# Rotary embedding on one core: all work in pairs of rows, and three PSUM banks for TensorE

## The chip, the core and the metric

The kernel runs on one core of a Trainium2 chip. The metric is the device time of one execution in microseconds (us); of several runs the median is given. The engines are TensorE (PE, its weight loads PEld), VectorE (DVE), ScalarE (ACT), GpSimd (POOL) and SyncE (SP), which here only issues transfers. Data come from and go to the chip's memory by sixteen DMA engines.

## What is computed

```python
def reference(x, cos, sin, num_heads):          # x: (16, 512, 1024), cos and sin: (512, 32), 16 heads
    batch, seq, dim = x.shape
    head_dim = dim // num_heads                 # 64
    half_dim = head_dim // 2                    # 32
    x = x.reshape(batch, seq, num_heads, head_dim)
    x1, x2 = (x[..., :half_dim].copy(), x[..., half_dim:].copy())
    cos = cos[None, :, None, :].copy()
    sin = sin[None, :, None, :].copy()
    return np.concatenate([x1 * cos - x2 * sin, x1 * sin + x2 * cos], axis=-1)
```

All is float32. Each element is used once: 33.6 MB are read and 33.6 MB written.

## The kernel before

The input is cut into eight tiles of 4 MB. A tile holds two batches: 128 partitions with eight rows of 1024 elements each (R = 8). Five buffers (`NB`, line 35) hold tiles, so the load of tile 5 goes into the buffer of tile 0 and has to wait until that one is stored.

In each row the result is x * cos + swapped(x) * signed sin, where "swapped" exchanges the two halves of each head. So a row costs two multiplications and an addition. The names in the code:

- `T` and `B` (line 157) are the second product, swapped(x) * sin. GpSimd makes nearly all of them; one is made by VectorE. `T1` and `T2` cover three rows each, `B` the remaining two.
- `P` (line 171) is the first product, x * cos, put by VectorE into a PSUM tile `pp`. `S` (line 174) adds the two, `T + pp`, back into the tile, also on VectorE.
- `A` (line 168) is the first product in place, for the two rows whose addition is left to TensorE. TensorE adds by multiplying both products with an identity matrix into one PSUM tile `ps` of 512 columns (lines 188 and 189), and ScalarE copies it back (line 190). One such step is called a chunk here; a pair of rows has four. Five tiles (`ONPE`) do so with their pair: twenty chunks. There is one bank `ps`, so a chunk begins when the copy of the one before is done.

The order is written out by hand: `GPO` for GpSimd, `DVO` for VectorE. `CARRY` and `AHEAD` add waits by hand, so that an engine's later instructions need none of their own, and the memset `both` (line 206) stands behind GpSimd's first `T` to carry the wait for the tables. The cosine and sine tables are spread over the partitions by a matmul each (line 117); cosine stays in PSUM (`cos_ps`).

All transfers of x are in SP's queue, in this order: the loads of tiles 0 to 4 (tile 0 in three pieces, tile 1 in two), the stores of tiles 0 to 2, the loads of tiles 5 to 7, the stores of tiles 3 to 7 (the last in two pieces). SP issues one after the other and waits at each for what it needs. The two tables are loaded from ScalarE's queue.

Of the kernel before, what the change touches and what calls it, by code (L numbers as in the profile page):

```python
# [7 lines left out]
FP32 = mybir.dt.float32  # L8
ALU = mybir.AluOpType
# [3 lines left out]
def kernel(  # L13
# [8 lines left out]
    nc = tc.nc  # L22
    P = nc.NUM_PARTITIONS
    batch, seq, dim = x.shape
    nh = num_heads
    hd = dim // nh
    half = hd // 2


    BP = 2  # L30
    HP = P // BP
    R = seq // HP
    NT = batch // BP
    assert HP * R == seq and BP * NT == batch
    NB = 5
    G = 3

    ROWS = {"1": (0, G), "2": (G, G), "pair": (2 * G, R - 2 * G)}

    LAST = {"pair": (0, R - 2 * G), "1": (R - 2 * G, G), "2": (R - G, G)}  # L40

    ONPE = (1, 3, 4, 5, 6)

    GPO = [("T1", "T2")] + [("B", "T1", "T2") if t in (2, 4, 7) else ("T1", "B", "T2") for t in range(1, NT)]

    DVO = [("P1", "S1", "P2", "B", "S2", "P3", "S3"), ("A", "P1", "S1", "P2", "S2"),
           ("P1", "S1", "P2", "S2", "P3", "S3"), ("A", "P1", "S1", "P2", "S2"), ("P1", "S1", "P2", "A", "S2"),
           ("P1", "S1", "P2", "A", "S2"), ("P1", "A", "S1", "P2", "S2"), ("P3", "S3", "P1", "S1", "P2", "S2")]

    CARRY = {(0, "P1"): "both", (0, "P2"): "T2", (1, "A"): "B", (3, "A"): "B", (4, "A"): "T2", (5, "P1"): "T1", (5, "A"): "T2",  # L50
             (6, "A"): "B", (7, "P3"): "B"}

    AHEAD = (1, 2, 3, 5)

    xv = x.rearrange("b (p r) d -> (b p) (r d)", r=R)
    xv = xv.rearrange("(t p) f -> t p f", p=P)
    ov = out.rearrange("b (p r) h d -> (b p) (r h d)", r=R)
    ov = ov.rearrange("(t p) f -> t p f", p=P)
# [2 lines left out]

    fixed = ctx.enter_context(tc.tile_pool(name="fixed", bufs=1))
    xin = ctx.enter_context(tc.tile_pool(name="xin", bufs=1))
    tpool = ctx.enter_context(tc.tile_pool(name="tpool", bufs=2))
    bpool = ctx.enter_context(tc.tile_pool(name="bpool", bufs=2))
    ptab = ctx.enter_context(tc.tile_pool(name="ptab", bufs=1, space=bass.MemoryType.PSUM))
    pgrp = ctx.enter_context(tc.tile_pool(name="pgrp", bufs=1, space=bass.MemoryType.PSUM))
    prow = ctx.enter_context(tc.tile_pool(name="prow", bufs=1, space=bass.MemoryType.PSUM))

    ctx.enter_context(tc.manual_schedule())  # L70

    SYNC = mybir.DependencyInfo(mybir.DependencyClass.Sync, mybir.DependencyReason.DATA)

    def implied(inst, *others):

        for o in others:
            tc.declare_no_dep(inst.ins, o.ins, reason="implied by an earlier wait of the engine")


    bufs = [xin.tile([P, R * dim], FP32, name=f"x{i}_sb") for i in range(NB)]  # L80
    x_tiles = [bufs[t % NB] for t in range(NT)]
    loads = [None] * NT
    stores = [None] * NT
    copies = [[] for _ in range(NT)]
    H = dim // 2

    def load(t, cuts=(0, 2 * R)):
        loads[t] = [nc.sync.dma_start(out=x_tiles[t][:, a * H:b * H], in_=xv[t][:, a * H:b * H])  # L88
                    for a, b in zip(cuts, cuts[1:])]

    def store(t, *parts):
        stores[t] = [nc.sync.dma_start(out=ov[t][:, a * H:b * H], in_=x_tiles[t][:, a * H:b * H])
                     for a, b in parts or ((0, 2 * R),)]

    load(0, (0, 1, 2 * G, 2 * R))
    tabs = fixed.tile([HP, 2, R * half], FP32, name="tabs")
    nc.scalar.dma_start(out=tabs[:, 1], in_=sinv)
    nc.scalar.dma_start(out=tabs[:, 0], in_=cosv)
    load(1, (0, 2 * G, 2 * R))
    for t in range(2, NB):  # L100
        load(t)


    ident = fixed.tile([P, P], FP32, name="ident")
    nc.gpsimd.memset(ident, 0.0)  # L105
# [6 lines left out]
    nc.gpsimd.tensor_copy(out=sel.rearrange("k (b p) -> k b p", b=BP),  # L112
                          in_=bass.AP(tensor=i64.tensor, offset=i64.offset, ap=[i64.ap[0], [0, BP], [1, HP]]))

    cos_ps = ptab.tile([P, R, half], FP32, name="cos_ps")
    sin_ps = pgrp.tile([P, G * dim], FP32, name="pp")[:, :R * half].rearrange("p (r j) -> p r j", r=R)
    spread = [nc.tensor.matmul(out=o.rearrange("p r j -> p (r j)"), lhsT=sel, rhs=tabs[:, i],  # L117
                               start=True, stop=True) for i, o in ((1, sin_ps), (0, cos_ps))]

    PR, PN = ROWS["pair"]  # L120
    sns = fixed.tile([P, R, 2, half], FP32, name="sns")
    snp = prow.tile([P, dim // 2], FP32, name="ps")
    signed = []
    for o, r0 in ((sns, 0), (snp[:, :PN * hd].rearrange("p (r s j) -> p r s j", r=PN, s=2), PR)):
        signed.append(nc.scalar.copy(out=o[:, :, 1, :], in_=sin_ps[:, r0:r0 + o.shape[1], :]))  # L125
        signed.append(nc.scalar.mul(out=o[:, :, 0, :], in_=sin_ps[:, r0:r0 + o.shape[1], :], mul=-1.0))  # L126

    def view(ap, r0, n):

        return ap[:, r0 * dim:(r0 + n) * dim]  # L130

    def cosb(r0, n):
        return bass.AP(tensor=cos_ps.tensor, offset=cos_ps.offset + r0 * half,
                       ap=[cos_ps.ap[0], [half, n], [0, 2 * nh], [1, half]])

    def snsb(tab, r0, n):

        return bass.AP(tensor=tab.tensor, offset=tab.offset + r0 * hd,
                       ap=[tab.ap[0], [hd, n], [0, nh], [1, hd]])

    def swapped(xt, r0, n):
        return bass.AP(tensor=xt.tensor, offset=xt.offset + r0 * dim + half,
                       ap=[xt.ap[0], [hd, n * nh], [-half, 2], [1, half]])

    Ts, TIs = {}, {}
    both = fixed.tile([1, 1], FP32, name="both")

    def span(t, o):
        return (LAST if t == NT - 1 else ROWS).get(o[-1]) or (LAST if t == NT - 1 else ROWS)["pair"]

    def second(eng, t, o):

        r0, n = span(t, o)
        pool = bpool if o == "B" else tpool
        Ts[t, o] = pool.tile([P, n * dim], FP32, name=o[0])
        tab = snsb(snp, r0 - PR, n) if eng is nc.vector else snsb(sns, r0, n)
        TIs[t, o] = eng.tensor_tensor(out=Ts[t, o], in0=swapped(x_tiles[t], r0, n), in1=tab, op=ALU.mult)  # L157
        return TIs[t, o]

    pps = {}  # L160

    def vector(t, o):
        r0, n = span(t, o)
        xr = view(x_tiles[t], r0, n)
        if o == "B":
            i = second(nc.vector, t, o)
        elif o == "A":
            i = nc.vector.tensor_tensor(out=xr, in0=xr, in1=cosb(r0, n), op=ALU.mult)  # L168
        elif o[0] == "P":
            pps[o[1]] = pgrp.tile([P, G * dim], FP32, name="pp")[:, :n * dim]  # L170
            i = nc.vector.tensor_tensor(out=pps[o[1]], in0=xr, in1=cosb(r0, n), op=ALU.mult)  # L171
        else:
            T = Ts[t, "B" if o == "S3" else "T" + o[1]]
            i = nc.vector.tensor_tensor(out=xr, in0=T, in1=pps[o[1]], op=ALU.add)  # L174
        if (t, o) in CARRY:
            after(i, TIs[t, CARRY[t, o]])
        implied(i, *loads[t], *spread, *signed)
        if t >= NB:
            implied(i, *loads[t - NB], *stores[t - NB], *copies[t - NB])
        return i  # L180

    def pe_rows(t):

        xr = view(x_tiles[t], PR, PN)
        for c in range(2 * PN):
            ps = prow.tile([P, dim // 2], FP32, name="ps")
            xc = xr[:, c * H:(c + 1) * H]
            nc.tensor.matmul(out=ps, lhsT=ident, rhs=xc, start=True, stop=False)  # L188
            nc.tensor.matmul(out=ps, lhsT=ident, rhs=Ts[t, "B"][:, c * H:(c + 1) * H], start=False, stop=True)  # L189
            i = nc.scalar.copy(out=xc, in_=ps)  # L190
            implied(i, *loads[t], *([As[t]] if t in As else []))
            if t >= NB:
                implied(i, *loads[t - NB], *stores[t - NB], *copies[t - NB])
            copies[t].append(i)

    def after(inst, other):
        tc.add_manual_dep(inst.ins, other.ins.name, SYNC, reason="brings the wait to the engines behind")

    As = {}

    def compute(t):
        for o in GPO[t]:
            i = second(nc.gpsimd, t, o)
            if (t, o) == (0, "T1"):

                TIs[0, "both"] = nc.gpsimd.memset(both, 0.0)  # L206
                after(TIs[0, "both"], signed[-1])
                after(TIs[0, "both"], spread[1])
        for o in DVO[t]:
            i = vector(t, o)  # L210
            if o == "A":
                As[t] = i
        if t in ONPE:
            pe_rows(t)

    for t in range(NB):
        compute(t)
# [5 lines left out]
        store(t)  # L223
    for t in range(NB, NT):
        compute(t)
        if t == NT - 1:
            store(t, (0, 2 * (R - G)), (2 * (R - G), 2 * R))
        else:
            store(t)
    for t in AHEAD:  # L230
        for l in loads[t + 1]:
            after(TIs[t, "T2"], l)


# [33 lines left out]
```

## Time and profile before

| | |
|---|---|
| median of three runs | 164.04 us (162.93 to 164.66) |
| span of the profiled execution | 162.0 us (no other time of this execution is given) |
| VectorE busy | 134.1 us, 83% |
| GpSimd busy | 138.9 us, 86% |
| TensorE busy | 54.6 us, 34%, 84 records |
| ScalarE busy | 14.0 us, 9% |
| DMA | 67.24 MB, mean 415 GB/s |

The span reaches from the first to the last instruction of one execution taken by the profiler. Busy times are sums of one engine's instructions; the engines work beside each other, so they don't add up to the span. A line of the profile's groups names the source line, the engine, the operation with its output and inputs, the shape, how often it ran, then its busy time, the mean of one in ns, and the idle time just before it.

### The profile page before, as it was taken

The numbers are of one execution on the slowest core, as the hardware profiler recorded it, in microseconds if no ns is written. First come the engines' busy times: TensorE is split into PE (matmuls) and PEld (weight loads), VectorE is DVE, ScalarE is ACT, GpSimd is POOL, SyncE is SP. The second block draws the span as 40 slices with busy tenths as digits, with TensorE's granted clock in tenths as the row PEclk, the third lists the DMA queues.
The fourth block names the chain that finished last, engine by engine and source line by source line (L and its number), as shares of the span: only waits on it lengthen the run. The fifth ranks groups of instructions, "written<-read, shape, count | busy, mean of one in ns | idle before, by whom it ended". The sixth has DMA issues, their size and how long they took to land.

```text
span 162.0 us, 381 instructions
## 1 busy us (share of the span) xinstructions
PE 54.6 (34%) x84; PEld 18.0 (11%) x84; DVE 134.1 (83%) x44; ACT 14.0 (9%) x25; POOL 138.9 (86%) x31
## 2 busy tenths in 40 slices
PE   0230000008680000038640009863988686400000
PEld 0110000002220000022110002220222132100000
DVE  0004999999999999999999999998968999999800
ACT  3200000000211000001210000021011212100000
POOL 2199999979999999999999999999999999992000
PEclk9999999999998555556995555599555899975555
DMA  6999999999999999998999999998999999799995
GB/s 190 392 456 403 425 496 388 461 445 388 461 445 388 404 502 388 421 485 388 429 453 396 445 461 396 461 437 372 453 445 404 396 396 453 332 388 518 384 409 243
DMA packets 3040, 67.24 MB, mean 415 GB/s; under 512 B 352, under 2 KB 480, under 8 KB 608
## 3 DMA queue, kind: packets, MB, share of 16 engines
q1 hardware_dynamic: 2880, 67.11, 97.2%
q10 hardware_dynamic: 160, 0.13, 0.2%
HBM read 33.69 MB, written 33.55 MB: 415 GB/s over the span
## 4 chain that ended last, share of the span: by engine, by line
DVE 33%; issue 26%; PE 19%; POOL 8%; ACT 4%; DMA 4%; SPq 0%; DVEq 0%; POOLq 0%
DVE x_sb L174 15%; DVE pp L171 13%; PE ps L188 11%; PE ps L189 9%; POOL T L157 6%; ACT x_sb L190 4%; DMA x_sb<-in_x_dram 4%; POOL B L157 3%; DVE x_sb L168 3%; DVE B L157 1%; SPq L88 0%; POOL both L206 0%; POOLq L157 0%; DVEq L174 0%; DVEq L171 0%
## 5 line engine op out<-in xcount | busy, mean ns | idle before, releaser
L157 POOL TENSOR_TENSOR T<-x_sb,sns 128x3072 f32<-128x3072 f32 x16 | 107.0, 6717 | 7.2 <-DMA x_sb<-in_x_dram 6.9
L171 DVE TENSOR_TENSOR pp<-x_sb,cos_ps 128x3072 f32<-128x3072 f32 (+1 forms) x19 | 60.7, 3193 | 15.2 <-POOL both L206 14.4
L188 PE MATMUL ps<-x_sb,ident 128*128 128x512 f32 x40 | 29.0, 815 | 76.6 <-issue 39.6
L174 DVE TENSOR_TENSOR x_sb<-T,pp 128x3072 f32<-128x3072 f32 x16 | 53.6, 3352 | 1.0
L157 POOL TENSOR_TENSOR B<-x_sb,sns 128x2048 f32<-128x2048 f32 x7 | 31.9, 4561 | 0.0
L189 PE MATMUL ps<-B,ident 128*128 128x512 f32 x40 | 26.7, 756 | 0.0
L190 ACT COPY x_sb<-ps 128x512 f32<-128x512 f32 x20 | 11.7, 585 | 121.9 <-PE ps L189 121.9
L188 PEld LDWEIGHTS ps<-x_sb,ident 128*128 128x128 f32 x40 | 7.4, 231 | 98.1 <-issue 68.8
L168 DVE TENSOR_TENSOR x_sb<-x_sb,cos_ps 128x2048 f32<-128x2048 f32 x5 | 11.4, 2285 | 2.8 <-POOL B L157 2.2
L189 PEld LDWEIGHTS ps<-B,ident 128*128 128x128 f32 x40 | 9.7, 241 | 13.4 <-issue 13.4
L174 DVE TENSOR_TENSOR x_sb<-B,pp 128x2048 f32<-128x2048 f32 x3 | 6.9, 2286 | 0.1
L117 PE MATMUL pp<-tabs,sel 64*128 64x256 f32 x2 | 1.2, 694 | 4.3 <-DMA tabs<-in_sin_dram 4.3
L117 PE MATMUL cos_ps<-tabs,sel 64*128 64x256 f32 x2 | 1.2, 713 | 4.1 <-DMA tabs<-in_cos_dram 4.1
L157 DVE TENSOR_TENSOR B<-x_sb,ps 128x2048 f32<-128x2048 f32 x1 | 2.3, 2281 | 0.0
L125 ACT ACT_TABLE_LOAD x1 | 1.3, 1283 | 1.9 <-issue 1.9
L117 PEld LDWEIGHTS cos_ps<-tabs,sel 64*128 64x128 f32 x2 | 0.5, 308 | 4.8 <-DMA tabs<-in_cos_dram 4.8
L117 PEld LDWEIGHTS pp<-tabs,sel 64*128 64x128 f32 x2 | 0.5, 310 | 4.3 <-issue 4.3
L125 ACT COPY sns<-pp 128x256 f32<-128x256 f32 x1 | 0.4, 372 | 2.3 <-PE pp L117 2.3
L105 POOL MEMSET ident<- 128x128 f32 x1 | 0.2, 204 | 0.3 <-POOLq L249 0.3
L126 ACT ACTIVATE sns<-pp 128x256 f32<-128x256 f32 x1 | 0.4, 390 | 0.0
L106 POOL TENSOR_SCALAR_AFFINE_SELECT ident<-ident 128x128 f32<-128x128 f32 x1 | 0.3, 292 | 0.1
L112 POOL COPY sel<-ident 64x128 f32<-64x128 f32 x1 | 0.3, 282 | 0.1
(7 smaller groups left out, 1.0 us busy)
## 6 DMA issues: line engine op xcount, KB each, us to landing
out_dram<-x_sb SPq DMA_DIRECT2D x7, 4096.0 KB, 20.5
x_sb<-in_x_dram SPq DMA_DIRECT2D x6, 4096.0 KB, 30.2
x_sb<-in_x_dram SPq DMA_DIRECT2D x2, 2560.0 KB, 16.4
out_dram<-x_sb SPq DMA_DIRECT2D x1, 2560.0 KB, 11.1
x_sb<-in_x_dram SPq DMA_DIRECT2D x1, 1536.0 KB, 15.2
out_dram<-x_sb SPq DMA_DIRECT2D x1, 1536.0 KB, 7.9
x_sb<-in_x_dram SPq DMA_DIRECT2D x1, 1280.0 KB, 6.3
x_sb<-in_x_dram SPq DMA_DIRECT2D x1, 256.0 KB, 3.0
```

Source lines behind the costliest of these rows:

```text
L106: nc.gpsimd.affine_select(out=ident, in_=ident, compare_op=ALU.not_equal, fill=1.0, base=0, pattern=[[-1, P]], channel_multiplier=1,)
L112: nc.gpsimd.tensor_copy(out=sel.rearrange("k (b p) -> k b p", b=BP), in_=bass.AP(tensor=i64.tensor, offset=i64.offset, ap=[i64.ap[0], [0, ...
L117: spread = [nc.tensor.matmul(out=o.rearrange("p r j -> p (r j)"), lhsT=sel, rhs=tabs[:, i], start=True, stop=True) for i, o in ((1, sin_ps ...
L125: signed.append(nc.scalar.copy(out=o[:, :, 1, :], in_=sin_ps[:, r0:r0 + o.shape[1], :]))
L126: signed.append(nc.scalar.mul(out=o[:, :, 0, :], in_=sin_ps[:, r0:r0 + o.shape[1], :], mul=-1.0))
L157: TIs[t, o] = eng.tensor_tensor(out=Ts[t, o], in0=swapped(x_tiles[t], r0, n), in1=tab, op=ALU.mult)
L168: i = nc.vector.tensor_tensor(out=xr, in0=xr, in1=cosb(r0, n), op=ALU.mult)
L171: i = nc.vector.tensor_tensor(out=pps[o[1]], in0=xr, in1=cosb(r0, n), op=ALU.mult)
L174: i = nc.vector.tensor_tensor(out=xr, in0=T, in1=pps[o[1]], op=ALU.add)
L188: nc.tensor.matmul(out=ps, lhsT=ident, rhs=xc, start=True, stop=False)
L189: nc.tensor.matmul(out=ps, lhsT=ident, rhs=Ts[t, "B"][:, c * H:(c + 1) * H], start=False, stop=True)
L190: i = nc.scalar.copy(out=xc, in_=ps)
```

## The change

Everything is done in pairs of rows (`G = 2`), four pairs in a tile, and one list `PLAN` holds the order for all engines. `T` is the second product on GpSimd, `B` the same on VectorE, `P` and `S` as before, `A` the first product in place and `M` the four chunks of a pair on TensorE with ScalarE's copies. Odd tiles give GpSimd three pairs and VectorE one `B`; even tiles from 2 on give GpSimd all four. Tiles 1 to 6 have two `M` each, tile 7 has one.

The second products share a ring of five buffers (`tpool`), the chunks a ring of three PSUM banks (`prow`). The cosine table and the part of the sine table that VectorE needs share one bank (`tab`). In a chunk the second product's matmul now stands ahead of the first's. The waits by hand (`CARRY`, `AHEAD`, `both`) are gone; each instruction waits for what it reads and overwrites.

Tile 0 is loaded in pieces of 2, 2 and 4 rows, the other tiles in one piece, and the last store is cut after six rows. The order of the transfers in SP's queue stays otherwise.

```diff
-    G = 3
-    ROWS = {"1": (0, G), "2": (G, G), "pair": (2 * G, R - 2 * G)}
-    ONPE = (1, 3, 4, 5, 6)
-    GPO = [("T1", "T2")] + [("B", "T1", "T2") if t in (2, 4, 7) else ("T1", "B", "T2") for t in range(1, NT)]
-    DVO = [("P1", "S1", "P2", "B", "S2", "P3", "S3"), ("A", "P1", "S1", "P2", "S2"),
...
+    G = 2
+    C = 512
+    PLAN = ["T0 P0 T1 S0 B3 P1 S1 T2 P3 S3 P2 S2",
+            "T0 T1 A0 M0 B3 T2 A1 M1 P3 S3 P2 S2",
+            "T0 T1 T2 T3 A0 M0 A1 M1 P2 S2 P3 S3",
+            "T0 T1 A0 M0 B3 T2 A1 M1 P3 S3 P2 S2",
+            "T0 T1 T2 T3 A0 M0 A1 M1 P2 S2 P3 S3",
+            "T0 T1 A0 M0 B3 T2 A1 M1 P3 S3 P2 S2",
+            "T0 T1 T2 T3 A0 M0 A1 M1 P2 S2 P3 S3",
+            "T0 T1 T2 A0 M0 B3 P1 S1 P2 S2 P3 S3"]
...
-    tpool = ctx.enter_context(tc.tile_pool(name="tpool", bufs=2))
-    bpool = ctx.enter_context(tc.tile_pool(name="bpool", bufs=2))
+    tpool = ctx.enter_context(tc.tile_pool(name="tpool", bufs=5))
...
-    prow = ctx.enter_context(tc.tile_pool(name="prow", bufs=1, space=bass.MemoryType.PSUM))
+    prow = ctx.enter_context(tc.tile_pool(name="prow", bufs=3, space=bass.MemoryType.PSUM))
...
-    load(0, (0, 1, 2 * G, 2 * R))
+    load(0, (0, 2))
...
-    load(1, (0, 2 * G, 2 * R))
-    for t in range(2, NB):
+    load(0, (2, 4), (4, 8))
+    for t in range(1, NB):
         load(t)
...
+        made = []
+        for c in range(G * dim // C):
+            ps = prow.tile([P, C], FP32, name="ps")
+            xc = xr[:, c * C:(c + 1) * C]
+            made.append(nc.tensor.matmul(out=ps, lhsT=ident, rhs=Ts[t, k][:, c * C:(c + 1) * C],
+                                         start=True, stop=False))
+            made.append(nc.tensor.matmul(out=ps, lhsT=ident, rhs=xc, start=False, stop=True))
+            made.append(nc.scalar.copy(out=xc, in_=ps))
+        return made
...
-        if t == NT - 1:
-            store(t, (0, 2 * (R - G)), (2 * (R - G), 2 * R))
-        else:
-            store(t)
-    for t in AHEAD:
-        for l in loads[t + 1]:
-            after(TIs[t, "T2"], l)
+        store(t, *((0, 6), (6, 8)) if t == NT - 1 else ())
```

More of the change, by code (lines that the diff above doesn't have):

```diff
@@ L33 @@
     NT = batch // BP
-    assert HP * R == seq and BP * NT == batch
     NB = 5
-    G = 3
-    ROWS = {"1": (0, G), "2": (G, G), "pair": (2 * G, R - 2 * G)}
-    LAST = {"pair": (0, R - 2 * G), "1": (R - 2 * G, G), "2": (R - G, G)}
-    ONPE = (1, 3, 4, 5, 6)
-    GPO = [("T1", "T2")] + [("B", "T1", "T2") if t in (2, 4, 7) else ("T1", "B", "T2") for t in range(1, NT)]
-    DVO = [("P1", "S1", "P2", "B", "S2", "P3", "S3"), ("A", "P1", "S1", "P2", "S2"),
[L47 to L53, printed above, removed]
+    G = 2
+    C = 512
+    assert HP * R == seq and BP * NT == batch and R == 4 * G
+    PLAN = ["T0 P0 T1 S0 B3 P1 S1 T2 P3 S3 P2 S2",
[7 rows of a table added]
     xv = x.rearrange("b (p r) d -> (b p) (r d)", r=R)
@@ L81, with load, store @@
     x_tiles = [bufs[t % NB] for t in range(NT)]
[L82 to L93, printed above, removed]
-    load(0, (0, 1, 2 * G, 2 * R))
+    loads = [[] for _ in range(NT)]
+    stores = [[] for _ in range(NT)]
+    def load(t, *cuts):
+        for a, b in cuts or ((0, R),):
+            loads[t].append(nc.sync.dma_start(out=x_tiles[t][:, a * dim:b * dim], in_=xv[t][:, a * dim:b * dim]))
+    def store(t, *cuts):
+        for a, b in cuts or ((0, R),):
+            stores[t].append(nc.sync.dma_start(out=ov[t][:, a * dim:b * dim], in_=x_tiles[t][:, a * dim:b * dim]))
+    load(0, (0, 2))
     tabs = fixed.tile([HP, 2, R * half], FP32, name="tabs")
@@ L113 @@
                           in_=bass.AP(tensor=i64.tensor, offset=i64.offset, ap=[i64.ap[0], [0, BP], [1, HP]]))
-    cos_ps = ptab.tile([P, R, half], FP32, name="cos_ps")
+    tab = ptab.tile([P, C], FP32, name="tab")
+    cos_ps = tab[:, :R * half].rearrange("p (r j) -> p r j", r=R)
+    snp = tab[:, R * half:R * half + G * hd].rearrange("p (r s j) -> p r s j", r=G, s=2)
+    BP0 = 3
     sin_ps = pgrp.tile([P, G * dim], FP32, name="pp")[:, :R * half].rearrange("p (r j) -> p r j", r=R)
@@ L118 @@
                                start=True, stop=True) for i, o in ((1, sin_ps), (0, cos_ps))]
-    PR, PN = ROWS["pair"]
     sns = fixed.tile([P, R, 2, half], FP32, name="sns")
-    snp = prow.tile([P, dim // 2], FP32, name="ps")
     signed = []
-    for o, r0 in ((sns, 0), (snp[:, :PN * hd].rearrange("p (r s j) -> p r s j", r=PN, s=2), PR)):
+    for o, r0 in ((sns, 0), (snp, BP0 * G)):
         signed.append(nc.scalar.copy(out=o[:, :, 1, :], in_=sin_ps[:, r0:r0 + o.shape[1], :]))
         signed.append(nc.scalar.mul(out=o[:, :, 0, :], in_=sin_ps[:, r0:r0 + o.shape[1], :], mul=-1.0))
-    def view(ap, r0, n):
-        return ap[:, r0 * dim:(r0 + n) * dim]
@@ L132, in cosb @@
[L132 to L171, printed above, removed]
-        else:
[L173 to L194, printed above, removed]
@@ L196, in after, with rows @@
-    def after(inst, other):
-        tc.add_manual_dep(inst.ins, other.ins.name, SYNC, reason="brings the wait to the engines behind")
-    As = {}
-    def compute(t):
[L202 to L214, printed above, removed]
+    def rows(t, k):
+        return x_tiles[t][:, k * G * dim:(k + 1) * G * dim]
@@ new lines, in cosb, with snb, swapped, emit @@
+    def cosb(k):
+        return bass.AP(tensor=cos_ps.tensor, offset=cos_ps.offset + k * G * half,
+                       ap=[cos_ps.ap[0], [half, G], [0, 2 * nh], [1, half]])
+    def snb(tab, k):
+        return bass.AP(tensor=tab.tensor, offset=tab.offset + k * G * hd, ap=[tab.ap[0], [hd, G], [0, nh], [1, hd]])
+    def swapped(xr):
+        return bass.AP(tensor=xr.tensor, offset=xr.offset + half, ap=[xr.ap[0], [hd, G * nh], [-half, 2], [1, half]])
+    Ts, pps = {}, {}
+    def emit(t, op):
+        o, k = op[0], int(op[1])
+        xr = rows(t, k)
+        if o in "TB":
+            Ts[t, k] = tpool.tile([P, G * dim], FP32, name="T")
+            eng, tb = (nc.gpsimd, snb(sns, k)) if o == "T" else (nc.vector, snb(snp, k - BP0))
+            return [eng.tensor_tensor(out=Ts[t, k], in0=swapped(xr), in1=tb, op=ALU.mult)]
+        if o == "P":
+            pps[t, k] = pgrp.tile([P, G * dim], FP32, name="pp")
+            return [nc.vector.tensor_tensor(out=pps[t, k], in0=xr, in1=cosb(k), op=ALU.mult)]
+        if o == "S":
+            return [nc.vector.tensor_tensor(out=xr, in0=Ts[t, k], in1=pps[t, k], op=ALU.add)]
+        if o == "A":
+            return [nc.vector.tensor_tensor(out=xr, in0=xr, in1=cosb(k), op=ALU.mult)]
+        made = []
[7 more added lines that the diff above has]
+        return made
@@ L216 @@
+    done = [[] for _ in range(NT)]
+    def compute(t):
+        for op in PLAN[t].split():
+            for i in emit(t, op):
+                if t and op[0] != "T":
+                    implied(i, *loads[t])
+                if t >= NB:
+                    implied(i, *loads[t - NB], *stores[t - NB], *done[t - NB])
+                done[t].append(i)
     for t in range(NB):
@@ L225 @@
         compute(t)
-        if t == NT - 1:
-            store(t, (0, 2 * (R - G)), (2 * (R - G), 2 * R))
-        else:
-            store(t)
-    for t in AHEAD:
-        for l in loads[t + 1]:
-            after(TIs[t, "T2"], l)
+        store(t, *((0, 6), (6, 8)) if t == NT - 1 else ())
 _INS = ['x', 'cos', 'sin', 'num_heads']
```

## The prediction

> **What bounds the kernel now.** I read the page's busy lines and DMA row first, then its groups, the landings of single transfers, short windows, and the chain of waits.
>
> ```profile
> span 162.0 us, 381 instructions
> PE 54.6 (34%) x84; PEld 18.0 (11%) x84; DVE 134.1 (83%) x44; ACT 14.0 (9%) x25; POOL 138.9 (86%) x31
> DMA  6999999999999999998999999998999999799995
> q1 hardware_dynamic: 2880, 67.11, 97.2%
> DVE 33%; issue 26%; PE 19%; POOL 8%; ACT 4%; DMA 4%; SPq 0%; DVEq 0%; POOLq 0%
> ```
>
> The chain of waits (last line) speaks of VectorE, but the DMA row is full from the second slice to the last but one: the transfers take 97.2% of sixteen engines' time. VectorE (134.1 us) and GpSimd (138.9 us) come close behind. So two limits lie within a few per cent of each other, and the question is which ends last. The landings of late stores tell (issue time in the first line of each pair, time to landing in the second):
>
> ```profile
> L92 SPq DMA_DIRECT2D out_dram<-x_sb x1: 344/344/344, 84.8 to 84.8; - x1
> DMA to landing us min/median/max: 37.5/37.5/37.5
> L92 SPq DMA_DIRECT2D out_dram<-x_sb x1: 332/332/332, 129.5 to 129.5; - x1
> DMA to landing us min/median/max: 12.1/12.1/12.1
> L92 SPq DMA_DIRECT2D out_dram<-x_sb x1: 332/332/332, 140.2 to 140.2; - x1
> DMA to landing us min/median/max: 11.2/11.2/11.2
> ```
>
> Tile 3's store lands at 84.8 + 37.5 = 122.3 us, tile 5's at 141.6, tile 6's at 151.4; read the same way, tile 4's lands at 131.9 and the two pieces of tile 7's at 157.4 and 161.1. So each 4 MB takes 9.6 to 9.8 us without a break. Yet tiles 5 and 6 are issued late, and the DMA engines show it:
>
> ```profile
> 81.50:107.00 25.50, 9.93 (x14) 3.21 (x13) 25.19 (x8) 1.76 (x3) 25.50 (x5) 0.60 1.00 432
> 128.50:129.75 1.25, 0.57 (x2) 0.19 (x2) 1.25 (x1) 0.58 (x1) 1.21 (x2) 1.00 0.37 157
> 139.40:140.40 1.00, 0.13 (x1) 0.00 (x0) 0.96 (x2) 0.58 (x1) 1.00 (x2) 1.00 0.16 66
> ```
>
> The last two columns are the DMA share and GB/s. In a full stretch 432 GB/s go through, which is 9.7 us for 4 MB. In the two short windows most engines stand idle: 0.63 x 1.25 + 0.84 x 1.0 = 1.6 us, because VectorE has not finished tiles 5 and 6. That the landings still come every 9.7 us means that a few engines are behind the others, never idle, and the slowest engine makes the landing. They fell behind earlier. The loads of tiles 5 to 7 should take 29.1 us after store 2 landed (68.8 + 13.3 = 82.1), but the last lands at 82.2 + 30.4 = 112.6, 1.4 us late; store 2 itself came 0.5 us late after store 1 (50.5 + 21.4 = 71.9). Both places are turns between storing and loading. So this execution is limited by the slowest DMA engines, and for the others by VectorE at 129.5 and 140.2 us.
>
> **The change, part by part.** The prices:
>
> ```profile
> L157 POOL TENSOR_TENSOR T<-x_sb,sns 128x3072 f32<-128x3072 f32 x16 | 107.0, 6717 | 7.2 <-DMA x_sb<-in_x_dram 6.9
> L157 POOL TENSOR_TENSOR B<-x_sb,sns 128x2048 f32<-128x2048 f32 x7 | 31.9, 4561 | 0.0
> L168 DVE TENSOR_TENSOR x_sb<-x_sb,cos_ps 128x2048 f32<-128x2048 f32 x5 | 11.4, 2285 | 2.8 <-POOL B L157 2.2
> L174 DVE TENSOR_TENSOR x_sb<-T,pp 128x3072 f32<-128x3072 f32 x16 | 53.6, 3352 | 1.0
> L174 DVE TENSOR_TENSOR x_sb<-B,pp 128x2048 f32<-128x2048 f32 x3 | 6.9, 2286 | 0.1
> L190 ACT COPY x_sb<-ps 128x512 f32<-128x512 f32 x20 | 11.7, 585 | 121.9 <-PE ps L189 121.9
> ```
>
> Every two-row operation has a row here: VectorE 2.29 us, GpSimd 4.56 us. The new plan has 9+7+6+7+6+7+6+8 = 56 VectorE operations, 128.2 us against 134.1, and 3+3+4+3+4+3+4+3 = 27 on GpSimd, 123.1 us against 138.9. TensorE gets two pairs in each of tiles 1 to 6 and one in tile 7, thirteen (not twelve) pairs of four chunks: 52 instead of 20, with 52 copies, 30.4 us of ScalarE. TensorE's price comes from the first two chunks in the chain of waits:
>
> ```profile
> 37.02 2.05 PE ps L188 x2
> 39.07 1.72 PE ps L189 x2
> 41.45 1.13 PE ps L188 x2
> 42.58 0.87 PE ps L189 x2
> 43.47 0.59 ACT x_sb L190
> ```
>
> At full granted clock a chunk is 1.13 + 0.87 = 2.00 us, at the half clock (5 in the PEclk row) 3.77. Today one bank makes each chunk wait for the copy. With three banks a chunk waits for the copy three before it, done long ago, so matmuls follow each other as the second here follows the first: 0.87 each, 1.74 a chunk, 7.0 a pair. No row shows more than two in a row, so the bounds are 1.74 and 2.00; I take 1.74, the row for a matmul with one ahead of it. The clock: a first burst ran at half clock for one chunk, later ones (at 97 and 113 us) for two and three, with 0.67 us holes for the copies between. A burst without holes should be full within two chunks: up to 2 x 1.7 = 3.4 us extra.
>
> Now the order. The cosine table's matmul ends at 9.60 + 1.22 = 10.82 us in the trace; VectorE starts at 14.39 only because of the memset "both", which goes. It starts at 10.9, up to 2 us later if the table lands later beside the new 1 MB first piece. At 2.32 us per operation with its gap, tile 0 (nine) ends at 31.8, tile 1 (seven) at 48, and the first of tile 1's two pairs is ready for TensorE at 34.1: pairs end at 34.1 + 7.0 + 3.4 = 44.5 and 51.5, tile 2's at 58.5 and 65.5, their last copy at 66.1. GpSimd's third tile waits for T buffers that TensorE still reads (first pair of tile 1): 44.5, then 4.6 us each, so the last product of tile 2 is there at about 58, still ahead of VectorE's use.
>
> SP's queue holds stores 0, 1, 2, then loads 5, 6, 7, then the rest; a late store 2 holds back load 5 as well. Stores are due when the DMA engines run dry: store 1 at 60 (issued at 52.1), store 2 at about 69.3 (today issued at 68.8 without a hole; now 66.1). This margin of 3 us is the smallest. Later: load 5 lands at 92.1, tile 5 is done by 112 (issued at 129.5 today), tile 6 by 128 (140.2), tile 7's first six rows at 142 to 144 (146.3), all at 147 (153.2). The removed manual waits (nine on VectorE, those on GpSimd) are within these numbers; VectorE and GpSimd go out of the end's path, hidden by the DMA.
>
> So what is gained is DMA time. (a) The two holes: 1.6 us, from 0 (the slowest engines had none) to 1.6 (none falls behind). I take 0.7, as the lag of 1.9 us arose at turns between loads and stores which stay. (b) Pieces: 22 transfers become 21, and all are whole rows of 8 KB. Tile 0's three pieces land at 1.6 + 12.0 = 13.6, where 1.2 (start) + 9.7 + about 1 (data to landing) gives 11.9; 0 to 1.5 of this may go, 0.4 taken, as the two tables remain. The two pieces of tile 1's load and of the last store cost under 0.2. Sum: 162.0 - 0.7 - 0.4 = 160.9 us of span. The page gives no time of its own for the profiled execution; the median run is 2.0 above the span (0.9 to 2.7 by the runs shown), so 162.9 us, 0.7% less.
>
> A rule against this: the Trainium skill's "TensorE: Matmul & The Clock Gate" (A second HAM failure mode: psum-queue depth-cycling) says that cycling through PSUM banks leaves short pauses that send the clock back and forth. In this trace the clock stayed full through pauses of 0.67 us in each 2.66 once it was up (105 to 112 us), so I follow the trace; by the rule the third rival below would be the likely one.
>
> **The rivals.** (1) The whole gain: the slow engines are chance, none falls behind, and 1.6 + 0.8 = 2.4 us go: 161.6. For it: other 4 MB steps are flat at 9.6 to 9.8. Against: two of three turns showed the lag. The same skill's "DMA: Bandwidth & Descriptors" (Latency and other measured facts) says that two of the sixteen engines are usually slower than the rest; a lag that belongs to engines speaks for my 0.7 or less, though its flat steps do not look like it.
>
> (2) TensorE late, slower than before. If a chunk costs 2.25 instead of 1.74 (waits at each bank, or half clock in a quarter of the time), tile 2 ends at 34.1 + 3 + 16 x 2.25 + 0.6 = 73.7, 4.4 us after the DMA runs dry, and 48 chunks in a row put tile 6 at 34.1 + 3 + 108 + 0.6 = 145.7 against 138.5 + 4.4, 2.8 more: 162.9 + 7.2, about 170; some of it would overlap, so 169. It decides from about 2.0 us a chunk (69.7 for store 2). For it: three bursts today ran two or three chunks at half clock. Against: those had holes.
>
> (3) The lag grows: each of the two turns costs 1.4 us more, now that no hole lets the engines close up: 163.6 + 2.8 = 166.4. The turns are the same, so little speaks for it.
>
> **How the numbers follow.** A measurement here tells about 1% from no change: 162.4 to 165.7. The forecast has 0.46 (own range 161.9 to 163.9; 0.42 within 1%, 0.04 faster), rival 1 0.29 (faster), rival 2 0.15 (slower), rival 3 0.10 (0.08 slower, 0.02 within). Faster 0.33, same 0.44, slower 0.23. The range from 161.3 leaves out little below; at 167.5 it holds rival 3 and mild forms of rival 2.
>
> **What would show it.** Right: DMA share about 1.0 from 4 to 158 us, none of the windows near 0.4; store 2 issued at 64 to 69; VectorE's last end near 147, several us ahead of the last landing; chunks 1.7 to 1.8 us; landings 9.7 us apart but for the turns. Wrong: a DMA hole near 70 us with VectorE or the copies named as what SP waited for (rival 2); landings over 10 us apart at turns (rival 3); a last landing before 159 (rival 1). The forecast as a whole falls if VectorE, GpSimd or TensorE still works when the last store should start.

## The result and the profile after

The changed kernel takes 164.49 us (median of 20 runs, 164.06 to 165.0). The kernel before took 162.91 us in 20 runs (162.76 to 164.7). The ratio is 1.0079, with a 95% interval of 1.0059 to 1.0099: 0.8% slower, where 0.7% faster was forecast. The difference lies inside the 1% that the prediction called no change, but this many runs tell it from nothing. Two of the three runs of before that the prediction started from (162.93, 164.04 and 164.66) were longer than usual. Among the 20 runs of before about a third lie above 163.3 us; they are called long here, and the rest, near 162.9, usual.

The page of the changed kernel, with the lines that answer to those shown of before. The one that decides is the fifth, a queue that carries instructions:

```profile
span 162.1 us, 696 instructions
PE 99.5 (61%) x212; PEld 41.7 (26%) x212; DVE 126.2 (78%) x56; ACT 32.8 (20%) x57; POOL 122.4 (76%) x34
DMA  5999999999999999999999999999999999999991
q1 hardware_dynamic: 2736, 67.11, 96.8%
q8 instruction: 1, 0.02, 0.0%
q14 instruction: 1, 0.01, 0.0%
```

VectorE and GpSimd are relieved as worked out (126.2 and 122.4 us of a span of 162.1), the DMA row is full to the last slice but one, and TensorE has 212 matmul records instead of 84. Queues q8 and q14, one transfer of instructions each, are new: the page of before has no such line.

Was compute early enough? The stores of tile 2, tile 6 and the last two rows (issue in the first line of each pair, time to landing in the second):

```profile
L83 SPq DMA_DIRECT2D out_dram<-x_sb x1: 332/332/332, 63.2 to 63.2; - x1
DMA to landing us min/median/max: 19.7/19.7/19.7
L83 SPq DMA_DIRECT2D out_dram<-x_sb x1: 333/333/333, 129.2 to 129.2; - x1
DMA to landing us min/median/max: 21.9/21.9/21.9
L83 SPq DMA_DIRECT2D out_dram<-x_sb x1: 333/333/333, 147.1 to 147.1; - x1
DMA to landing us min/median/max: 13.7/13.7/13.7
```

Store 2 is issued at 63.2 us (66.1 forecast, due at 69.3), tile 6's at 129.2 (128), the last at 147.1 (147); tile 5's, not shown, at 114.9 (112). Each waits in the queue far longer than its data take, so nothing is late for the transfers any more. The timeline of TensorE's first burst (start, duration, engine, line) shows that its chunks were priced rightly:

```profile
40.04 1.02 PE L150 MATMUL ps<-T,ident 128*128 128x512 f32 x2
40.90 1.02 PE L152 MATMUL ps<-x_sb,ident 128*128 128x512 f32 x2
41.76 1.02 PE L150 MATMUL ps<-T,ident 128*128 128x512 f32 x2
```

The starts lie 0.86 us apart, so a chunk of two takes 1.72 us (1.74 forecast).

All the same the span ends at 162.1 us. The stretches just before the end (its bounds and length, the five engines' busy times, granted clock, DMA share, GB/s):

```profile
158.50:159.50 1.00, 0.00 (x0) 0.00 (x0) 0.00 (x0) 0.00 (x0) 0.00 (x0) 0.50 0.16 66
159.50:161.00 1.50, 0.00 (x0) 0.00 (x0) 0.00 (x0) 0.00 (x0) 0.00 (x0) 0.50 0.05 22
```

A share of 0.16 is two or three of sixteen DMA engines (0.16 x 16 = 2.6), and 0.05 is less than one. The rest are done. The packet records of the trace say it engine by engine. (They name no engine; packets that follow one another without a gap are taken as one engine's.) The fastest ends at 158.3, thirteen of the sixteen by 158.8, then 159.1 and 159.8, the last at 160.5. Each transfer leaves sixteen end records, and each engine moves about 4.2 of the 67.1 MB, so no engine takes over another's share, and the last one sets the landing.

That last engine's records show where it fell back. From 71.3 us it carries, between two packets of data, the q8 transfer: 16,384 bytes, 0.92 us. Its next 32 KB packet takes 1.62 us instead of 1.21. So it falls 1.3 us further behind, and it loses 0.6 more at 109 to 111 us, where the queue turns from loads to stores. It has no idle time in which to catch up. The transfer comes when TensorE has begun 89 matmul records and 90 weight loads. The kernel before has 84 of each in all.

### The profile page after: what moved, and what is told of

It reads as the page before. It is cut to its first block, busy times and chain, and to the rows that moved or that the text cites. A ratio compares the mean times of both kernels' runs of the same rounds, so it can differ in the third digit from the quotient of the medians.

```text
span 162.1 us, 696 instructions
## 1 busy us (share of the span) xinstructions
PE 99.5 (61%) x212; PEld 41.7 (26%) x212; DVE 126.2 (78%) x56; ACT 32.8 (20%) x57; POOL 122.4 (76%) x34
## 3 DMA queue, kind: packets, MB, share of 16 engines
q1 hardware_dynamic: 2736, 67.11, 96.8%
## 4 chain that ended last, share of the span: by engine, by line
POOL 32%; DMA 31%; issue 12%; DVE 10%; POOLq 4%; SPq 1%; DVEq 0%
POOL T L138 32%; DMA x_sb<-in_x_dram 31%; DVE x_sb L143 4%; DVE pp L141 4%; POOLq L209 4%; DVE T L138 1%; SPq L79 1%; POOLq L138 0%; DVEq L143 0%; DVE x_sb L145 0%
## 5 line engine op out<-in xcount | busy, mean ns | idle before, releaser
L138 POOL TENSOR_TENSOR T<-x_sb,sns 128x2048 f32<-128x2048 f32 x27 | 121.4, 4532 | 14.5 <-DMA x_sb<-in_x_dram 7.9
L150 PE MATMUL ps<-T,ident 128*128 128x512 f32 x104 | 56.9, 630 | 23.8 <-POOL T L138 23.8
L152 PE MATMUL ps<-x_sb,ident 128*128 128x512 f32 x104 | 56.0, 620 | 6.8 <-DVE x_sb L145 6.8
L141 DVE TENSOR_TENSOR pp<-x_sb,tab 128x2048 f32<-128x2048 f32 x19 | 43.6, 2293 | 10.3 <-ACT tab L115 10.0
L153 ACT COPY x_sb<-ps 128x512 f32<-128x512 f32 x52 | 30.5, 586 | 97.4 <-PE ps L152 97.4
L143 DVE TENSOR_TENSOR x_sb<-T,pp 128x2048 f32<-128x2048 f32 x19 | 43.4, 2287 | 2.4 <-DVE pp L141 0.5
L145 DVE TENSOR_TENSOR x_sb<-x_sb,tab 128x2048 f32<-128x2048 f32 x13 | 29.4, 2281 | 8.1 <-POOL T L138 8.1
L150 PEld LDWEIGHTS ps<-T,ident 128*128 128x128 f32 x104 | 20.5, 200 | 51.0 <-POOL T L138 26.7
L152 PEld LDWEIGHTS ps<-x_sb,ident 128*128 128x128 f32 x104 | 20.2, 199 | 35.9 <-issue 22.2
L138 DVE TENSOR_TENSOR T<-x_sb,tab 128x2048 f32<-128x2048 f32 x5 | 11.4, 2280 | 0.0
```

The costliest lines, as they stand in the source:

```text
L138: return [eng.tensor_tensor(out=Ts[t, k], in0=swapped(xr), in1=tb, op=ALU.mult)]
L141: return [nc.vector.tensor_tensor(out=pps[t, k], in0=xr, in1=cosb(k), op=ALU.mult)]
L143: return [nc.vector.tensor_tensor(out=xr, in0=Ts[t, k], in1=pps[t, k], op=ALU.add)]
L145: return [nc.vector.tensor_tensor(out=xr, in0=xr, in1=cosb(k), op=ALU.mult)]
L150: made.append(nc.tensor.matmul(out=ps, lhsT=ident, rhs=Ts[t, k][:, c * C:(c + 1) * C], start=True, stop=False))
L152: made.append(nc.tensor.matmul(out=ps, lhsT=ident, rhs=xc, start=False, stop=True))
```

## The experiments

Three theories stood against each other. **A**: TensorE's longer instruction stream makes one DMA engine fetch 16 KB of instructions in the middle, and in a kernel with full DMA engines that time is never made up. **B**: nothing of TensorE matters; engines fall behind at the turns between loads and stores (the prediction's third rival), in the changed kernel more, as no hole lets them close up or as the pieces of tiles 0 and 1 start them otherwise. **C**: it is TensorE's and ScalarE's doubled traffic itself that slows transfers.

**The kernel before, profiled again.** No edit; one execution.

> The kernel before, unchanged, for a second profile of it. Twenty runs of it gave 162.8 to 164.7 us, most of them near 162.9, so the profile shown (span 162.0, about 2.0 under its time) was one of the longer ones. Theory A (refill: TensorE's longer instruction stream is fetched by one DMA engine in the middle of the kernel, which then is 1.3 us behind for good): a typical run of the kernel before has a slowest DMA engine less than 1.3 us behind the fastest at the end, a span of 160.8 to 161.2 and no instruction transfer within the span. Theory B (turns between loads and stores put single engines behind, in both kernels alike): the slowest engine is 2 us or more behind here too, span near 162.

Measured: 164.72 us, span 162.3. It was again a long execution: no instruction transfer, but its DMA engines end 2.3 us apart (158.67 to 160.96), having lost step at the turns at 80 to 82 and 109 to 111 us. So B's mechanism exists. The two stretches that were holes in the execution of the prediction, here:

```profile
128.50:129.75 1.25, 1.15 (x3) 0.67 (x4) 1.25 (x1) 0.05 (x1) 1.25 (x2) 1.00 1.15 498
139.40:140.40 1.00, 0.00 (x0) 0.00 (x0) 0.96 (x2) 0.00 (x0) 1.00 (x2) 0.50 0.99 426
```

There is no hole (a share above 1 comes from packets that start in the window and end behind it), and yet the span is no shorter. In the prediction's execution the engines were 2.3 us apart up to the end of tile 4's store at 131.6 us; in the holes the leading ones waited, and all ended within 0.2 us of each other, the last at 160.73. So the holes cost that execution nothing. Whether engines usually lose step like this is the next question.

**Two more executions of before.**

> The kernel before once more, for a profile of one of its usual executions (span 160.4 to 160.6 in most of its runs, against 162.0 and 162.3 in the two profiles so far). If what made those two longer was single DMA engines falling behind at the turns between loads and stores (2.3 us between the fastest and the slowest at the end of both), a usual execution has its engines about 0.5 to 1 us apart at the end. If it was VectorE's late stores at 129.5 and 140.2 us, a usual execution has these stores 1 us or more earlier and the engines as far apart as before.

> As the run beside it: a second chance of a usual execution of the kernel before, with the same expectations.

Measured: 162.97 us (span 160.5) and 162.78 us (span 160.3), both close to the median. From the page of the second its span, then its store of tile 5 and the stretch just before its end:

```profile
span 160.3 us, 381 instructions
```

```profile
L92 SPq DMA_DIRECT2D out_dram<-x_sb x1: 332/332/332, 124.3 to 124.3; - x1
DMA to landing us min/median/max: 15.6/15.6/15.6
```

```profile
158.50:159.50 1.00, 0.00 (x0) 0.00 (x0) 0.00 (x0) 0.00 (x0) 0.00 (x0) 0.50 0.01 0
```

Tile 5's store is issued at 124.3, not at 129.5 as in the execution that the prediction read, and waits 15.6 us in the queue: the holes at 128.5 and 139.4 us do not exist here. Its DMA engines end between 158.31 and 158.94, 0.6 us apart, and behind 158.5 next to no packet starts. So the first expectation came true, and of the second one's two signs only the earlier stores. The usual execution of the kernel before was already at the limit of its transfers, with nothing to gain but the 0.6.

**Only the longer instruction stream.** The kernel before, with forty one-column matmuls on TensorE ahead of tile 1's chunks:

```diff
     def pe_rows(t):
+        if t == 1:
+            ps = prow.tile([P, dim // 2], FP32, name="ps")
+            for _ in range(40):
+                nc.tensor.matmul(out=ps[:1, :1], lhsT=ident[:, :1], rhs=ident[:, :1], start=True, stop=True)
```

> The kernel before with 40 matmuls of one column added on TensorE ahead of tile 1's chunks, where TensorE is idle; they add some 160 instructions to its stream and nothing to the work of other engines. Theory A: an instruction transfer of 16 KB shows up near 41 us, one DMA engine falls behind by 1.3 us, and the time goes up by 0.8 to 1.6 us (ratio 1.005 to 1.010). Theory B: no change (0.998 to 1.002).

Measured: 165.34 us (165.18 to 165.46), ratio 1.0141 (1.0121 to 1.0161). The page:

```profile
span 162.7 us, 542 instructions
PE 54.5 (33%) x164; PEld 19.6 (12%) x164; DVE 134.1 (82%) x44; ACT 14.0 (9%) x25; POOL 138.9 (85%) x31
q8 instruction: 1, 0.02, 0.0%
```

TensorE is as busy as before (54.5 us), and the other engines' work is unchanged. Only the records went from 84 to 164, and q8 appears. The fetch runs at 41.2 us, with TensorE at 89 records; one DMA engine goes from 0.7 to 2.1 us behind, to 2.8 at the next turn, and ends at 161.4 while all others end by 159.0. That is A, without anything else of the change. The loss, 2.36 us against the 162.98 us of the kernel before beside it, is more than the 0.8 to 1.6 us expected, which had left out the loss at the turn.

**Fewer instructions in the changed kernel, most else kept.** One bfloat16 matmul for each chunk, of the upper halves of the second product; the first product is left out of these rows. A float32 matmul leaves two matmul records and two weight loads, a bfloat16 one leaves one of each:

```diff
+    identb = fixed.tile([P, P], mybir.dt.bfloat16, name="identb")
+    nc.gpsimd.tensor_copy(out=identb, in_=ident)
...
-            made.append(nc.tensor.matmul(out=ps, lhsT=ident, rhs=Ts[t, k][:, c * C:(c + 1) * C],
-                                         start=True, stop=False))
-            made.append(nc.tensor.matmul(out=ps, lhsT=ident, rhs=xc, start=False, stop=True))
+            hi = Ts[t, k].bitcast(mybir.dt.bfloat16)[:, 2 * c * C + 1:2 * (c + 1) * C:2]
+            made.append(nc.tensor.matmul(out=ps, lhsT=identb, rhs=hi, start=True, stop=True))
```

> The changed kernel with one bf16 matmul per chunk instead of two float32 ones: the rows added by TensorE get only the second product, rounded (the first product's part is left out), so that TensorE's stream has 104 instructions for the chunks instead of 416. Transfers, VectorE and GpSimd stay as in the changed kernel. Theory A: no instruction transfer within the span, the slowest engine about 0.9 us behind, 162.6 to 163.3 us (ratio to before 0.998 to 1.003). Theory B: as the changed kernel, 164.2 to 164.9 (1.006 to 1.010).

Measured: 162.76 us (162.73 to 162.88), ratio 0.9983 (0.997 to 0.9995). No q8, and from its page and its windows:

```profile
span 160.7 us, 386 instructions
PE 28.8 (18%) x56; PEld 6.7 (4%) x56; DVE 126.2 (79%) x56; ACT 29.1 (18%) x57; POOL 122.4 (76%) x35
```

```profile
158.50:159.50 1.00, 0.00 (x0) 0.00 (x0) 0.00 (x0) 0.00 (x0) 0.00 (x0) 1.00 0.08 33
```

VectorE and GpSimd work as in the changed kernel, ScalarE nearly so (29.1 us instead of 32.8), and the DMA engines end 0.9 us apart. The 1.73 us to the changed kernel could still be TensorE's traffic (theory C), so the stream was lengthened again.

**The same, with the forty one-column matmuls added** ahead of tile 1's first chunk (first product left out as above):

```diff
+        if (t, k) == (1, 0):
+            ps = prow.tile([P, C], FP32, name="ps")
+            for _ in range(40):
+                made.append(nc.tensor.matmul(out=ps[:1, :1], lhsT=ident[:, :1], rhs=ident[:, :1], start=True, stop=True))
```

> The changed kernel with one bf16 matmul per chunk (the first product's part of those rows left out, which alone gave 162.76 us), and 40 matmuls of one column ahead of tile 1's first chunk, which add 160 instructions to TensorE's stream and no work that anyone waits for. Theory A: a 16 KB instruction transfer comes back at about 35 to 45 us, one engine falls 1.3 us behind and loses more at the turns: 164.0 to 165.3 us (1.006 to 1.014). Theory C (the half precision run was fast because TensorE reads and ScalarE waits less): no change, 162.6 to 163.1 us.

Measured: 164.67 us (164.33 to 165.0), ratio 1.008 (1.0054 to 1.0107): all of the loss is back, 1.91 us, with TensorE 30.7 us busy.

```profile
q8 instruction: 1, 0.02, 0.0%
```

The fetch runs at 32.5 us (1.09 us, the next packet 1.69). This engine ends at 161.4, all others by 159.1. Theory C falls.

**One float32 matmul for each chunk.** The first product is left out, so that the fetch should come much later:

```diff
             made.append(nc.tensor.matmul(out=ps, lhsT=ident, rhs=Ts[t, k][:, c * C:(c + 1) * C],
-                                         start=True, stop=False))
-            made.append(nc.tensor.matmul(out=ps, lhsT=ident, rhs=xc, start=False, stop=True))
+                                         start=True, stop=True))
```

> The changed kernel with one float32 matmul per chunk instead of two (the first product's part of those rows is left out): TensorE works half as much and has 208 instructions for the chunks. In the changed kernel the transfer of instructions came when TensorE had done 88 matmul records and 88 weight loads. Theory A: the same number is reached here at about 110 to 120 us, the instruction transfer comes then, and the time stays near the changed kernel's (1.005 to 1.010). If TensorE's or ScalarE's traffic were the cause (theory C), halving TensorE's work would lower the time to about half way, 1.003 to 1.005. Theory B: 1.006 to 1.010.

Measured: 163.49 us (162.71 to 163.92, without one execution of 168.8), ratio 1.0015 (0.999 to 1.0039). The fetch comes at 123.6 us, with TensorE at 85 records, and puts its engine 0.95 us further behind (0.75 to 1.70). The profiled execution was the one of 168.8 us, so only the place and duration of the fetch are read from it. The place was right, the size was not: A expected a ratio of 1.005 to 1.010, and the time is only 0.73 us above the version without a fetch. No turn between loads and stores follows, so what a lagging engine lost at turns in the other kernels (0.6 to 1.2 us) is missing here; that this is the reason is inferred, as there is no trace of an execution of usual length.

**The full computation without the 16 KB fetch.** The changed kernel with one pair on TensorE in tiles 1, 3, 4, 5 and 6 only, as before; GpSimd makes all second products from tile 1 on:

```diff
-            "T0 T1 A0 M0 B3 T2 A1 M1 P3 S3 P2 S2",
-            "T0 T1 T2 T3 A0 M0 A1 M1 P2 S2 P3 S3",
...
+            "T0 T1 T2 T3 A0 M0 P1 S1 P2 S2 P3 S3",
+            "T0 T1 T2 T3 P0 S0 P1 S1 P2 S2 P3 S3",
...
-                if t and op[0] != "T":
+                if t and op[0] not in "TP":
```

> The changed kernel with one pair on TensorE in each of tiles 1, 3, 4, 5 and 6 instead of thirteen pairs: twenty chunks as before, 60 operations on VectorE (137 us) and 31 on GpSimd (141 us), nothing left out. Theory A (refill): TensorE's stream is as short as in the kernel before, no 16 KB instruction transfer, the slowest DMA engine 0.9 us or less behind; GpSimd's last product at about 150 us and the last store issued at about 153, just in time: 162.6 to 163.3 us (0.998 to 1.003). Theory B (turns between loads and stores): as the changed kernel, 164.1 to 165.0. A third possibility: GpSimd is now so full that the last stores come late, 163.5 to 165, with DMA holes in the last 25 us.

Measured: 163.23 us (162.87 to 163.61), ratio 0.9993 (0.9968 to 1.0019), 1.26 us below the changed kernel.

```profile
span 161.0 us, 416 instructions
PE 54.4 (34%) x84; PEld 20.2 (13%) x84; DVE 136.6 (85%) x60; ACT 14.0 (9%) x25; POOL 140.0 (87%) x38
q14 instruction: 1, 0.01, 0.0%
```

There are 84 records and no q8. VectorE and GpSimd are 10 and 18 us busier than in the changed kernel, and it is still faster: their relief bought nothing, and what the thirteen pairs add on TensorE cost 1.3 us. The q14 line is 8 KB of another queue, which the changed kernel has too. Here it runs at 100.3 us and takes 0.31 us, its engine's next packet takes 1.82, and that engine ends last, at 159.7, 0.5 us behind the next: the same cost on a smaller scale.

**The changed kernel with before's pieces** (tile 0 in 0.5, 2.5 and 5 rows, tile 1 in 3 and 5):

```diff
-    load(0, (0, 2))
+    load(0, (0, 0.5), (0.5, 3), (3, 8))
...
-    load(0, (2, 4), (4, 8))
-    for t in range(1, NB):
+    load(1, (0, 3), (3, 8))
+    for t in range(2, NB):
```

> The changed kernel with the pieces of before: tile 0 in 0.5, 2.5 and 5 rows, tile 1 in 3 and 5. In the profiles the sixteen engines are 0.4 us apart after the changed kernel's first loads and 0.8 us after the ones before, and the engines that are behind lose more where loads turn into stores. If this start matters: the lag grows and the time rises by 0.2 to 0.8 us over the changed kernel. If only the refill matters: 164.2 to 164.8 us, as the changed kernel.

Measured: 164.41 us (163.66 to 164.87), ratio 1.0063 (1.0036 to 1.0089), 0.08 us from the changed kernel. The fetch is there (71.7 us, 1.04 us long), and its engine ends at 161.3, 1.8 us behind the next. The pieces do not make the difference.

**The kernel before with fewer pieces** (tile 0 in 3 and 5 rows, tile 1 in one):

```diff
-    load(0, (0, 1, 2 * G, 2 * R))
+    load(0, (0, 2 * G, 2 * R))
...
-    load(1, (0, 2 * G, 2 * R))
-    for t in range(2, NB):
+    for t in range(1, NB):
```

> The kernel before with tile 0 loaded in two pieces of 3 and 5 rows and tile 1 in one. If the small pieces make the spread of the engines at the start, and that spread makes the long executions of the kernel before (163.2 to 164.7 us in about a third of them): median 162.5 to 162.9 us with fewer long ones. If not: 162.8 to 163.1 with as many long ones. VectorE starts no later: GpSimd's first product waits for 3 rows either way.

Measured: 165.16 us (164.87 to 165.41), ratio 1.0102 (1.0063 to 1.0142). This expectation missed. No fetch, and the sixteen engines keep together (they end between 160.78 and 161.25), but all lose time at the turns: packets of 1.4 to 2.3 us instead of 1.21 at 80 to 83 us, and of 1.3 to 1.9 at 109 to 112. By the ends of the same transfers in the usual execution every engine loses about 2.0 us at the first and 0.5 at the second. So a turn can cost all engines time, and what a turn costs is not set by how far apart the engines started, as I had thought. VectorE also started later (it waited 16.7 us for the memset `both`, 14.4 in the execution shown). Which of these moves the turns stays open.

The fetches in one table (place, duration and the next packet from the packet records; "behind" is the last engine's end against the fastest's):

| kernel | records, PE | fetch at, us | took | next 32 KB packet | behind at the end | median |
|---|---|---|---|---|---|---|
| before, usual | 84 | none | | | 0.6 | 162.91 |
| bfloat16 chunks | 56 | none | | | 0.9 | 162.76 |
| five pairs on TensorE | 84 | none of 16 KB | | | 0.8 | 163.23 |
| one float32 matmul a chunk | 108 | 123.6 | 0.96 | 1.60 | not read | 163.49 |
| changed kernel | 212 | 71.3 | 0.92 | 1.62 | 2.2 | 164.49 |
| changed, before's pieces | 212 | 71.7 | 1.04 | 1.59 | 2.9 | 164.41 |
| bfloat16 chunks + 40 matmuls | 135 | 32.5 | 1.09 | 1.69 | 3.0 | 164.67 |
| before + 40 matmuls | 164 | 41.2 | 1.09 | 1.69 | 2.9 | 165.34 |

## Why the prediction was wrong, step by step

**What bounds the kernel: half right.** "This execution is limited by the slowest DMA engines" held for that execution, and full transfers are the limit in all. But it was a long execution. The spans of the two usual ones are 160.3 and 160.5, not 162.0. What made it long were the turns, as the prediction read; the holes were where the engines that had not fallen behind waited.

**"So what is gained is DMA time": this step failed.** Term (a), 0.7 us for the two holes, and term (b), 0.4 us for the pieces, were sized on losses that the usual execution does not have. (a) is 0: tile 5's store is issued at 124.3 in a usual execution of before and is not waited for, and the long execution without holes ends no earlier than the one with them (160.96 against 160.73). (b) is 0 too: tile 0's data are in at 13.2 us in the prediction's execution and at 13.3 in the changed kernel, the fastest DMA engine ends at 158.31 in the usual before and in the changed kernel, and giving the old pieces back moved the time by 0.08 us. The spread of the three runs, 162.93 to 164.66, was in sight, and I put the holes of the one profile against their median without asking which kind of execution it was. Without the fetch (bfloat16 chunks, 162.76 us) the time is that of before: the forecast of 162.9 us was, by luck, the usual time of the kernel before and of the changed one without its fetch.

**The missing term.** The prediction priced the 52 chunks by their matmuls' durations and put their instructions at nothing: 212 matmul records and as many weight loads. The sum lacked one fetch: 0.92 us + 0.41 on the next packet = 1.3 us on one DMA engine, and with the turn after it 1.9. The runs with and without a fetch differ by 1.73 us (the changed kernel against the bfloat16 chunks), 1.91 (these with and without the added matmuls) and 2.36 (the kernel before with and without them). "Hidden by the DMA" was said of VectorE's and GpSimd's work, and it is true of them; what TensorE's work costs the DMA itself was not asked.

A page of the Trainium skill, "Runtime: NRT & Kernel Launch" (Instruction fetch mechanics), says that instructions are refilled in blocks of 16 KiB by a DMA queue of the engine's own, and that crossing a block is mostly hidden. The trace agrees with the block: 16,384 bytes each time on q8. It disagrees with the price: 1.7 to 2.4 us of the time here where a turn followed, since the fetch takes its turn on an engine that has no idle time.

**"The median run is 2.0 above the span": wrong for before.** Time less span is 2.4 to 2.5 us in four executions of before (164.72 - 162.3, 162.97 - 160.5, 162.78 - 160.3, and 165.18 - 162.7 with the added matmuls), and 1.9 to 2.3 in the changed kernel and its variants, but for one run with 3.1. So the changed kernel gains about 0.4 us outside the span and loses about 2.0 inside (median spans of 162.45 and, in the 23 executions of before that ran beside the first experiments, 160.5); the 1.6 measured is the difference. The 2.0 fits the changed kernel, but by luck. What the 0.4 is was not tried.

**Right.** The chunk at 1.72 us; VectorE, GpSimd and TensorE out of the end's path; the stores' issue times to 3 us; no wait for TensorE at 70 us. So rival 2 (TensorE late, 169 us) did not happen. One reading was wrong without harm: the slow first chunk at 37 us was not at half granted clock, which is 1.00 from 36 to 40 us; in the changed kernel too the first chunk takes 2.99 us (35.33 to 38.32) at a granted clock of 1.00. Why is open. The rule on pauses between PSUM banks, cited against the change, did not come true either (where the prediction says that it would lead to the third rival, a slow TensorE is the second): the granted clock is 9 tenths or more in every slice up to 93 us, dips to 8, 5 and 8 tenths between 93 and 105 us, where TensorE had paused for a slice, and is full again until the bursts end; its mean is 0.912. Rival 1 (161.6) had the flat steps right, but there were no holes to win back; the two slower DMA engines set against it do not show in the usual execution, where all sixteen end within 0.6 us. Rival 3 had the right place, the slowest engine at the end, and in part the right size: 0.6 us at one turn. The cause was another.

**Not settled.** Why some executions of before lose about 1.7 us at the turns, and what in a turn stretches packets from 1.21 to 2.3 us. The fetch comes when 85 to 89 matmul records have begun; which instruction starts it is not known.

## What to carry to other kernels

Where the DMA engines are full, everything that moves by DMA counts, instructions too: count the instructions that a change adds to an engine, even a nearly idle one, and read the page's queues for a new line of kind "instruction". Read the end of a transfer-limited kernel from its slowest DMA engine (DMA shares of 0.16 and 0.05 just before the end here), not from the mean share, which was 96.8% here and 97.2% and 97.8% in two executions of before. And ask first whether the profiled execution is a usual one: a hole seen in a long execution is no gain in the median.

## What the hardware showed that I had not expected

- A fetch of 16 KB takes 0.92 to 1.09 us on one DMA engine and stretches that engine's next 32 KB packet from 1.21 to between 1.59 and 1.69 us. It came at 85 to 89 of TensorE's matmul records in five kernels, wherever these lay in time (32.5 to 123.6 us).
- Where a turn between loads and stores lies behind the fetch, the engine that is behind lost 0.6 to 1.2 us more there, in four kernels; where none does, the time was 0.73 us above the version without a fetch.
- Turns can cost all sixteen engines time together: packets of up to 2.3 us instead of 1.21, in the kernel before with fewer pieces.
